# Input sums for the seven products read from an unsplit DRAM copy, two portions per step, in a macaron network on one Trainium2 core

## The chip, the cores and the metric

The kernel runs on one core of a Trainium2 chip. The metric is the device time of one execution in microseconds; lower is better. The engines appear under the names of the profile: PE (TensorE) multiplies, DVE (VectorE), ACT (ScalarE) and POOL (GpSimd) do elementwise work, SP (SyncE) issues most of the transfers, each engine in the order of its own instruction list.

## What is computed

Two layers over 512 tokens with a context of 256 tokens in front, 1024 features, all in fp32. Each layer is a gated FFN, a mixer, and a second gated FFN; each of the three is wrapped in a residual, a layer norm and a modulation by shift, scale and gate vectors. The mixer of layer 0 is a bidirectional gated linear attention plus a windowed pooling, that of layer 1 a differential attention.

```python
def ffn_substep(x, mods, w_in, w_out, g, b):
    shift, scale, gate = mods
    y = swiglu(modulate(x, shift, scale), w_in, w_out)
    return layer_norm(ALPHA * x + MACARON * gate * y, g, b)
def swiglu(h, w_in, w_out):
    a, b = jnp.split(h @ w_in, 2, axis=-1)
    return (jax.nn.silu(a) * b) @ w_out
```

w_in is 1024 x 5632 and w_out 2816 x 1024. The first three FFNs see 768 tokens, the last one only the 512 of the sequence.

## The kernel before, in words

The program is, in this order: FFN 1, the even mixer, FFN 2, FFN 3, the odd mixer, FFN 4. Features lie on the 128 partitions in 8 blocks, tokens along the free axis.

**Three matmuls for one product.** Every fp32 operand is split into a high part and a remainder, both in the fast fp32r form (`split`, L117 on ACT for the high part, L119 mostly on DVE, at some places on POOL, for the remainder), and `mm3` (L157 to L159) multiplies high by high, high by low, low by high. The tiles `xh`, `xl` hold the split input of the running stage.

**The FFN's input projection.** The 2816 hidden features make 11 double blocks. The first `plain` ones (4 with 768 tokens, 5 with 512) go through `project`, two units each, where PE multiplies all 8 feature blocks in the ordinary way: a first group of units together with the last steps of the layer norm before, then the rest one by one, and beside each of these the generator `after` is moved on by one step. The remaining blocks go through `seven`, a Strassen-like scheme: 7 products of half-size operands in place of 8, 84 matmuls per block with 384 or 256 columns. Its operands are sums of weight quarters (POOL, L669 to L680, then split on ACT and DVE) and sums of input quarters. The latter are what `after` makes, in 4 portions (`sums_of_inputs`, L634): three POOL adds put xh and xl together again (tiles `b`, L646), five DVE subtractions form the sums (L644, the first of them twice because xh and xl are subtracted one after the other), and three of the sums are split into the tiles `six` (ACT and DVE). No block can go through `seven` beyond its first product before all four portions are there.

**The output projection and the layer norm** (`out_phase`, `layer_norm`) treat the tokens in two halves. While PE runs half 1, the norm of half 0 is moved on between its steps: two `mean` calls (each sums two accumulators by two matmuls with a matrix of 1/1024, L476), a reciprocal root, and then for each of the 8 blocks j a multiplication on DVE (L329), the modulated `h` (ACT L336 and POOL L338), its split into xh and xl, and the residual kept for the next stage (POOL L344) and stored (SP). At the same time ACT and DVE split the output weights of half 1 (`spare<-raw`). The norm of half 1 is moved on in the next stage's `project`.

**Order.** A scheduler puts each engine's instructions in order when the kernel is built; buffers come from pools, and a transfer or an operation waits until its buffer is free.

Of the kernel before, what the change touches and what calls it, by code (L numbers as in the profile page):

```python
# [12 lines left out]
F32 = mybir.dt.float32  # L13
# [6 lines left out]
P = 128  # L20
D = 1024
KB = D // P
NCTX = 256
NLAT = 512
NT = NCTX + NLAT
# [17 lines left out]
class Net:  # L43
    def __init__(self, tc, ctx, ins, out):
        self.tc, self.nc, self.ins, self.out = tc, tc.nc, ins, out
        self.ctx = ctx
        nc = self.nc
        pool = lambda name, bufs, **k: ctx.enter_context(tc.tile_pool(name=name, bufs=bufs, **k))
        self.const = pool("const", 1)
        self.stream = pool("stream", 1)  # L50
        self.lnp = pool("lnp", 1)
        self.n = 0
        self.psum_cm = None
        self.open_psum(h=7, st=1)
# [12 lines left out]
        self.ones_d = c.tile([P, P], F32, name="ones_d")  # L67
        nc.vector.memset(self.ones_d, 1.0 / D)
        self.eps_ln = c.tile([P, 1], F32, name="eps_ln")
        nc.vector.memset(self.eps_ln, LN_EPS)  # L70
        self.eps_rms = c.tile([P, 1], F32, name="eps_rms")
        nc.vector.memset(self.eps_rms, RMS_EPS)
        self.ident = c.tile([P, P], F32, name="ident")
        make_identity(nc, self.ident)
        self.ln = c.tile([P, DEPTH, 3, 2, KB], F32, name="ln")
        self.bada = c.tile([P, DEPTH, N_MOD * KB], F32, name="bada")
        nc.scalar.dma_start(out=self.bada, in_=ins["b_ada"])
        nc.scalar.dma_start(out=self.ln, in_=ins["ln"])
        self.lb = self._lower_bound(c, self._load(c, "hg_lb", [P, 8]))
        self.RB = None  # L80
        self.ax = None
        self.mod = [
            [c.tile([P, N_MOD * KB], F32, name=f"mod_{l}_{v}") for v in range(2)] for l in range(DEPTH)
        ]
        self.c_bc = self.c_act = self.settled = None
# [138 lines left out]
    def start(self, pool):  # L224
# [33 lines left out]

        w = lambda q: [load(self.ins["w_ada0"][q, i]) for i in range(KB // 2)]
# [6 lines left out]
        for j in range(KB):  # L266
# [8 lines left out]
            self.split(self.xh[:, j, :], self.xl[:, j, :], x_)  # L275
            if j % 2 and q < 4:
                columns(q, quarter)
# [21 lines left out]
    def layer_norm(self, half, halves, aff, nxt, ax_new, r_of, s1, done, table):  # L299
        nc = self.nc  # L300
# [6 lines left out]
        pm = self.mean(s1, n)  # L307
# [12 lines left out]
        pv = self.mean(s2, n)  # L320
# [6 lines left out]
        for j in range(KB):  # L327
            r = r_of(half, j)
            nc.vector.tensor_mul(out=r, in0=r, in1=rs[:, :n])  # L329
            if nxt is not None:  # L330
# [8 lines left out]
                self.split(self.xh[:, j, c0:c1], self.xl[:, j, c0:c1], h[:, :n])  # L339
            g, b = aff[:, 0, j:j + 1], aff[:, 1, j:j + 1]  # L340
# [27 lines left out]
    def out_phase(self, pool, nk, wsrc, gload, halves, gate, l, i, nxt, r_of, table=None, keep=False, ada=iter(())):  # L368
# [5 lines left out]
        if nxt is not None:  # L374
            self.n += 1
            ax_new = self.dram.tile([P, KB, NT], F32, name=f"ax{self.n}")
        nh = nk // 2
# [95 lines left out]
    def mean(self, s, n):  # L473
        ps = self.ps("st")[:, :n]
        for i in range(2):
            self.nc.tensor.matmul(out=ps, lhsT=self.ones_d, rhs=s[i], start=i == 0, stop=i == 1)  # L476
        return ps

    def residual(self, r, j, c0, c1):
# [5 lines left out]
        nc.scalar.mul(out=r, in_=r, mul=ALPHA)  # L485

# [6 lines left out]
    def project(self, ws, halves, ps_of, done, group, early=None, spare=None, after=None):  # L493
# [40 lines left out]
        for x in range(group, len(ws)):  # L534
            w = ahead.pop(0)
            if after:
                next(after, None)
# [15 lines left out]
    def ffn(self, l, p, halves, nxt, ada=((), ()), table=None, first_of_all=False):  # L553
# [5 lines left out]
        plain = 4 if n > 512 else 5  # L559
        in_ada, out_ada = (list(a) for a in ada)  # L560
        with ExitStack() as st:
# [72 lines left out]
            def sums_of_inputs():  # L634

                t1 = [self.spare(pool)[:, :2 * m].rearrange("p (k c) -> p k c", k=2) for _ in range(2)]
# [3 lines left out]
                for k in range(4):  # L640
                    hi = lambda K, N: B(K, N)[0][:, k, :].bitcast(F32)
                    lo = lambda K, N: B(K, N)[1][:, k, :].bitcast(F32)
                    b12, b22, b21 = (self.tmp("b")[:, :m] for _ in range(3))
                    sub = lambda o, a, b: nc.vector.tensor_sub(out=o, in0=a, in1=b)  # L644
                    for t, q in ((b12, (0, 1)), (b22, (1, 1)), (b21, (1, 0))):
                        nc.gpsimd.tensor_add(out=t, in0=hi(*q), in1=lo(*q))  # L646
                    if k == 1:
                        made["next"] = ahead(plain, room(plain))
                    a = t1[k // 2][:, k % 2, :]
                    sub(a, b12, hi(0, 0))  # L650
                    sub(a, a, lo(0, 0))
# [125 lines left out]
    def even_mixer(self, nxt):  # L777
# [5 lines left out]
        with ExitStack() as st:  # L783
# [14 lines left out]
            def proj_head(h, group):  # L798
                tiles = {}
                kinds = ("ff", "fb", "q", "g")  # L800
                cols = (12 + h, 16 + h, h, 8 + h)
# [39 lines left out]
            def gla(h):  # L841
# [4 lines left out]
                q, sg, F = d["q"], d["g"], d["f"]  # L846
# [129 lines left out]
                nc.vector.tensor_mul(out=rec, in0=rec, in1=sg)  # L976
# [51 lines left out]
            for h in range(H):  # L1028
                gla(h)
                if h + 1 < H:  # L1030
                    proj_head(h + 1, 0)
            proj_u()
        self.open_psum(h=7, st=1)
        self.mixer_out(8, ins["w_out_even"], mixd, halves, (0, 5), 0, 1, nxt, (0, 1, 2, 3, 6, 7, 4, 5))
# [336 lines left out]
```

## Time and profile before

| | us |
|---|---|
| median of 3 runs | 2773.55 (2772.56 to 2774.47) |
| the profiled execution | 2768.34 |
| its span | 2766.6 |
| granted TensorE clock, mean | 0.991 |

The times of all rows below are of the profiled execution, counted from the start of its span; it lies 5.2 us below the median, and 1.7 us of its time are outside the span. The profile gives for every engine when it was busy, and in square brackets the idle time in front of an instruction with what ended it.

### The profile page before, as it was taken

The page shows a single profiled execution, that of the slowest core. Times are in us where ns is not written, and L with a number is a line of the kernel's source. Part 1 is how long each engine was busy: PE and PEld are TensorE (multiplying, and loading weights), DVE is VectorE, ACT ScalarE, POOL GpSimd, SP SyncE. Part 2 cuts the span into 40 slices and gives each one's busy share as a digit, 9 for nine tenths or more (in the row PEclk, how much of TensorE's full clock was granted, in tenths as well). Part 3 has the DMA queues.
Part 4 walks back from the last instruction along what each step waited for, and adds up shares of the span by engine and source line. Part 5 has one row for each costly group of instructions (what it writes and reads, how often), then busy time and mean ns, then how long its engine had stood idle before and what let it go on. Part 6 is the DMA issues. An engine that isn't in the chain of part 4 may idle for free.

```text
span 2766.6 us, 43965 instructions
## 1 busy us (share of the span) xinstructions
PE 2669.8 (97%) x17396; PEld 2430.9 (88%) x17396; DVE 1957.9 (71%) x2905; ACT 1215.3 (44%) x1918; POOL 897.0 (32%) x686
## 2 busy tenths in 40 slices
PE   8999999999999899999999999999999998999997
PEld 6999988987787789998898999988887777989997
DVE  4899677757774679977786775556727786677665
ACT  3433433544552533443354444423534555545553
POOL 1555300522110554440054544201422211465302
PEclk9999999999999999999999999999999999999998
DMA  6344266521114334426653432265521113323563
GB/s 257 130 144 134 92 234 232 192 99 64 45 38 167 108 115 146 140 92 225 217 202 131 155 124 77 103 220 199 187 77 46 39 35 100 126 93 119 176 213 117
DMA packets 138770, 374.20 MB, mean 135 GB/s; under 512 B 16066, under 2 KB 47170, under 8 KB 138564
## 3 DMA queue, kind: packets, MB, share of 16 engines
q1 hardware_dynamic: 136832, 370.21, 38.2%
q8 instruction: 136, 2.23, 0.3%
q10 hardware_dynamic: 1732, 1.20, 0.1%
q14 instruction: 70, 0.57, 0.1%
HBM read 337.78 MB, written 33.56 MB: 134 GB/s over the span
## 4 chain that ended last, share of the span: by engine, by line
PE 75%; DVE 11%; ACT 5%; POOL 4%; issue 3%; DMA 1%; SPq 0%; POOLq 0%; ACTq 0%; DVEq 0%
PE ps L157 22%; PE ps L158 22%; PE ps L159 22%; DVE r4l L119 1%; PE ps L1237 1%; PE ps L1238 1%; PE ps L1239 1%; DVE spare L644 1%; DVE b L644 1%; ACT r4h L117 1%; PE ps L1208 1%; PE ps L476 1%; PE pss L1136 1%; DVE spare L119 1%; POOL b L646 1%
## 5 line engine op out<-in xcount | busy, mean ns | idle before, releaser
L117 ACT CAST r4h<-raw 128x1024 fp32r<-128x1024 f32 (+1 forms) x322 | 332.6, 1035 | 626.0 <-PE ps L158 318.7
L157 PE MATMUL ps<-xh,r4h 128*128 128x512 f32 (+2 forms) x1732 | 583.2, 338 | 12.1 <-ACT xh L117 8.3
L159 PE MATMUL ps<-xh,r4l 128*128 128x512 f32 (+2 forms) x1732 | 579.4, 335 | 0.0
L158 PE MATMUL ps<-xl,r4h 128*128 128x512 f32 (+2 forms) x1732 | 578.6, 334 | 0.7 <-DVE xl L119 0.7
L119 DVE TENSOR_TENSOR r4l<-raw,r4h 128x1024 fp32r<-128x1024 f32 (+1 forms) x306 | 371.0, 1213 | 229.2 <-ACT r4h L117 168.3
L157 PEld LDWEIGHTS ps<-xh,r4h 128*128 128x128 f32 x1732 | 326.3, 189 | 42.5 <-ACT xh L117 11.5
L158 PEld LDWEIGHTS ps<-xl,r4h 128*128 128x128 f32 x1732 | 326.7, 189 | 22.8 <-DVE xl L119 2.8
L159 PEld LDWEIGHTS ps<-xh,r4l 128*128 128x128 f32 x1732 | 326.9, 189 | 20.7 <-issue 0.5
L157 PE MATMUL ps<-six,r4h 128*128 128x384 f32 (+1 forms) x852 | 279.8, 328 | 13.9 <-ACT c L708 13.8
L158 PE MATMUL ps<-six,r4h 128*128 128x384 f32 (+1 forms) x852 | 277.2, 325 | 0.0
L159 PE MATMUL ps<-six,r4l 128*128 128x384 f32 (+1 forms) x852 | 276.5, 325 | 0.0
L157 PE MATMUL ps<-r4h 128*128 128x512 f32 (+1 forms) x768 | 276.5, 360 | 0.0
L159 PE MATMUL ps<-r4h,r4l 128*128 128x512 f32 (+1 forms) x768 | 275.6, 359 | 0.2
L158 PE MATMUL ps<-r4l,r4h 128*128 128x512 f32 (+1 forms) x768 | 275.5, 359 | 0.0
L157 PE MATMUL ps<-r4h,spare 128*128 128x256 f32 (+1 forms) x896 | 263.6, 294 | 2.7 <-ACT spare L117 2.7
L159 PE MATMUL ps<-r4h,spare 128*128 128x256 f32 (+1 forms) x896 | 260.5, 291 | 4.2 <-DVE spare L119 4.1
L158 PE MATMUL ps<-r4l,spare 128*128 128x256 f32 (+1 forms) x896 | 260.6, 291 | 0.0
L680 POOL TENSOR_TENSOR raw<-raw,late 128x512 f32<-128x512 f32 x71 | 96.6, 1361 | 427.7 <-DVE r4l L119 427.7
L119 DVE TENSOR_TENSOR r4l<-late,r4h 128x1024 fp32r<-128x1024 f32 x71 | 105.7, 1489 | 121.4 <-PE ps L158 107.8
L159 PEld LDWEIGHTS ps<-r4h,spare 128*128 128x128 f32 x896 | 172.9, 193 | 7.7 <-DVE spare L119 5.4
L185 DVE SCALAR_TENSOR_TENSOR trash<-spare 128x1024 bf16<-128x1024 f32 x112 | 178.9, 1599 | 0.4 <-DMA spare<-in_w_ada 0.4
L157 PEld LDWEIGHTS ps<-r4h,spare 128*128 128x128 f32 x896 | 173.0, 193 | 7.0 <-ACT spare L117 3.3
(288 smaller groups left out, 5648.3 us busy)
## 6 DMA issues: line engine op xcount, KB each, us to landing
raw<-in_w_ffn_in SPq DMA_DIRECT2D x176, 512.0 KB, 3.5
raw<-in_w_ffn_out SPq DMA_DIRECT2D x176, 512.0 KB, 4.2
spare<-in_w_ada SPq DMA_DIRECT2D x80, 512.0 KB, 5.2
six<-in_w_ada SPq DMA_DIRECT2D x64, 512.0 KB, 5.6
g<-late_g SPq DMA_DIRECT2D x88, 128.0 KB, 2.1
six<-g SPq DMA_DIRECT2D x44, 256.0 KB, 4.5
raw<-in_w_in_even SPq DMA_DIRECT2D x20, 512.0 KB, 3.5
raw<-in_w_in_odd SPq DMA_DIRECT2D x16, 512.0 KB, 3.5
```

The costliest lines, as they stand in the source:

```text
L117: self.copied = self.nc.scalar.copy(out=h, in_=src)
L119: eng.tensor_sub(out=l, in0=src, in1=h.bitcast(F32))
L157: mm(out=ps, lhsT=h, rhs=xh, start=first, stop=False)
L158: mm(out=ps, lhsT=h, rhs=xl, start=False, stop=False)
L159: mm(out=ps, lhsT=l, rhs=xh, start=False, stop=last)
L185: nc.vector.scalar_tensor_tensor(out=self.tmp("trash").bitcast(BF16), in0=r, scalar=1.0, in1=self.c_bc[v], op0=ALU.mult, op1=ALU.mult, acc ...
L476: self.nc.tensor.matmul(out=ps, lhsT=self.ones_d, rhs=s[i], start=i == 0, stop=i == 1)
L644: sub = lambda o, a, b: nc.vector.tensor_sub(out=o, in0=a, in1=b)
L646: nc.gpsimd.tensor_add(out=t, in0=hi(*q), in1=lo(*q))
L680: nc.gpsimd.tensor_sub(out=a12, in0=a12, in1=sums[:, 512:])
L1136: mm(out=ps[:, half, :384], lhsT=Q[halfs[m], i, qs], rhs=K[halfs[m], j, ks], start=x == 0, stop=x == 2)
L1208: mm(out=po[:, qs], lhsT=v[:, c, h * P:(h + 1) * P], rhs=t[:, c, :], start=c == 0, stop=c == NC - 1)
```

## The change

FFN inputs get an unsplit copy in DRAM (`whole`), written by SP where the input is split: at the start, and in `layer_norm` behind each split of `h` (ahead of the store of the residual). `sums_of_inputs` reads its quarters back from it, 16 transfers per FFN, so that the 48 POOL adds and one DVE subtraction of each portion fall away. `project` moves `after` on by two steps per unit. `plain` falls by one, so one more block of each FFN goes through `seven`. `mean` adds the two accumulators on DVE first in the norm of half 0, and uses one matmul there. In the even mixer the gate projection of the last head comes after the pooling's projections, its gating is a function of its own, and the order in which the output projection takes its inputs is changed.

```diff
-        for i in range(2):
-            self.nc.tensor.matmul(out=ps, lhsT=self.ones_d, rhs=s[i], start=i == 0, stop=i == 1)
+        if not last:
+            self.nc.vector.tensor_add(out=s[0], in0=s[0], in1=s[1])
+            s = s[:1]
+        for i, part in enumerate(s):
+            self.nc.tensor.matmul(out=ps, lhsT=self.ones_d, rhs=part, start=i == 0, stop=i == len(s) - 1)
...
                 self.split(self.xh[:, j, c0:c1], self.xl[:, j, c0:c1], h[:, :n])
+                if whole is not None:
+                    nc.sync.dma_start(out=whole[:, j, c0:c1], in_=h[:, :n])
...
-            if after:
-                next(after, None)
+            for _ in range(2):
+                next(after or iter(()), None)
...
-        plain = 4 if n > 512 else 5
+        plain = 3 if n > 512 else 4
...
-                    for t, q in ((b12, (0, 1)), (b22, (1, 1)), (b21, (1, 0))):
-                        nc.gpsimd.tensor_add(out=t, in0=hi(*q), in1=lo(*q))
+                    for t, (K, N) in ((a, (0, 0)), (b12, (0, 1)), (b22, (1, 1)), (b21, (1, 0))):
+                        nc.sync.dma_start(out=t, in_=self.whole[:, K * 4 + k, cols[N]])
...
-                    sub(a, b12, hi(0, 0))
-                    sub(a, a, lo(0, 0))
+                    sub(a, b12, a)
...
                 if h + 1 < H:
-                    proj_head(h + 1, 0)
+                    gate(h)
+                if h + 2 < H:
+                    proj_head(h + 1, 0)
+                elif h + 1 < H:
+                    proj_head(h + 1, 0, ("ff", "fb", "q"))
             proj_u()
+            proj_head(H - 1, 0, ("g",))
+            gate(H - 1)
```

What the scheduler makes of it is seen in the engines' lists. First DVE in FFN 2, where the first group of units has ended; `raw`, `late`, `r4l`, `r4s` belong to the weights of the next seven-product blocks. Before:

```order
L119 TENSOR_TENSOR r4l<-raw,r4h 128x1024
L583 TENSOR_TENSOR late_g<-sil,ps 128x256 x2
L644 TENSOR_TENSOR spare<-b,xh 128x384 x2
L644 TENSOR_TENSOR spare<-spare,xl 128x384
L644 TENSOR_TENSOR b<-b 128x384
L644 TENSOR_TENSOR spare<-spare,xl 128x384
L644 TENSOR_TENSOR b<-b,spare 128x384
L119 TENSOR_TENSOR six<-b,six 128x384
L644 TENSOR_TENSOR b<-b 128x384
L119 TENSOR_TENSOR six<-b,six 128x384
L644 TENSOR_TENSOR b<-b 128x384
L119 TENSOR_TENSOR six<-b,six 128x384
```

The same place of the changed kernel, where L658 is the line of the subtractions and L593 and L597 are the gating:

```order
L119 TENSOR_TENSOR r4l<-raw,r4h 128x1024
L597 TENSOR_TENSOR late_g<-sil,ps 128x256 x2
L119 TENSOR_TENSOR r4l<-late,r4h 128x1024
L119 TENSOR_TENSOR r4s<-raw,r4s 128x512
L658 TENSOR_TENSOR spare<-b,spare 128x384
L119 TENSOR_TENSOR r4l<-raw,r4h 128x1024
L658 TENSOR_TENSOR b<-b 128x384
L658 TENSOR_TENSOR b<-b,spare 128x384
L658 TENSOR_TENSOR spare<-b,spare 128x384
L119 TENSOR_TENSOR six<-b,six 128x384
L658 TENSOR_TENSOR b<-b 128x384
L119 TENSOR_TENSOR six<-b,six 128x384
```

One block's weight splits are now in front of the input sums instead of in the middle, the sums are one subtraction shorter, and the `spare` of the sums holds a loaded quarter.

Next POOL at the same place of FFN 2, with `late`, `raw` for the weight sums. Before:

```order
L669 TENSOR_TENSOR late<-raw 128x512
L670 TENSOR_TENSOR late<-late,raw 128x512
L671 TENSOR_TENSOR raw<-raw 128x512
L646 TENSOR_TENSOR b<-xh,xl 128x384 x6
L680 TENSOR_TENSOR raw<-raw,late 128x512
L669 TENSOR_TENSOR late<-raw 128x512
L670 TENSOR_TENSOR late<-late,raw 128x512
L671 TENSOR_TENSOR raw<-raw 128x512
L646 TENSOR_TENSOR b<-xh,xl 128x384 x6
L119 TENSOR_TENSOR xl<-spare,xh 128x384 x4
```

And in the changed kernel (L681 to L692 are the weight sums, L119 the remainder of the fourth sum):

```order
L681 TENSOR_TENSOR late<-raw 128x512
L682 TENSOR_TENSOR late<-late,raw 128x512
L683 TENSOR_TENSOR raw<-raw 128x512
L692 TENSOR_TENSOR raw<-raw,late 128x512
L681 TENSOR_TENSOR late<-raw 128x512
L682 TENSOR_TENSOR late<-late,raw 128x512
L683 TENSOR_TENSOR raw<-raw 128x512
L119 TENSOR_TENSOR xl<-spare,xh 128x384 x2
L681 TENSOR_TENSOR late<-raw 128x512
L682 TENSOR_TENSOR late<-late,raw 128x512
L119 TENSOR_TENSOR xl<-spare,xh 128x384
L683 TENSOR_TENSOR raw<-raw 128x512
```

The runs of six adds of xh and xl are gone, and the weight sums of two blocks and the splits into `xl` have moved up into their place.

Last ACT in the output projection of FFN 3, half 1, where the norm's blocks (`xh<-h`) and the split of the output weights (`spare<-raw`) alternate. Before, from the first `xh` on:

```order
L117 CAST xh<-h 128x512
L336 ACTIVATE h<-six,aff 128x256 x2
L117 CAST xh<-h 128x512 x2
L336 ACTIVATE h<-six,aff 128x256
L117 CAST spare<-raw 128x1024
L117 CAST xh<-h 128x512
L336 ACTIVATE h<-spare,aff 128x256 x2
L117 CAST xh<-h 128x512 x2
L336 ACTIVATE h<-spare,aff 128x256
L117 CAST spare<-raw 128x1024
L117 CAST xh<-h 128x512
L117 CAST spare<-raw 128x1024
```

And in the changed kernel, from its first `xh` on:

```order
L117 CAST xh<-h 128x512 x2
L338 ACTIVATE h<-six,aff 128x256 x2
L117 CAST xh<-h 128x512 x2
L117 CAST spare<-raw 128x1024
L338 ACTIVATE h<-spare,aff 128x256
L117 CAST xh<-h 128x512
L338 ACTIVATE h<-spare,aff 128x256 x2
L117 CAST xh<-h 128x512 x2
L117 CAST spare<-raw 128x1024 x2
L338 ACTIVATE h<-spare,aff 128x256
L117 CAST r4h<-six 128x512
L117 CAST xh<-h 128x512
```

The second of the weight splits in this stretch stood behind the sixth `xh` and now stands behind the seventh; the first has moved from behind the third to behind the fourth.

## Rows read from the trace of the kernel before

**Rows 1.** the page, busy time, share and instructions by engine

```profile
PE 2669.8 (97%) x17396; PEld 2430.9 (88%) x17396; DVE 1957.9 (71%) x2905; ACT 1215.3 (44%) x1918; POOL 897.0 (32%) x686
```

**Rows 2.** PE timeline, end of the plain units in FFN 1: start, duration, instruction

```profile
94.39 0.40 PE L157 MATMUL ps<-xh,r4h 128*128 128x512 f32 x1
...
95.45 0.34 PE L157 MATMUL ps<-xh,r4h 128*128 128x384 f32 x1
95.62 0.34 PE L158 MATMUL ps<-xl,r4h 128*128 128x384 f32 x1
```

**Rows 3.** windows, PE: length, busy time (matmuls), clock, DMA share, GB/s

```profile
2460.00:2480.00 20.00, 20.00 (x169) 1.00 0.34 119
```

**Rows 4.** waits of PE: total us, times, longest

```profile
PE ps L476 <- DVE acc L471: 9.2, 5, 4.3
...
PE ps L1008 <- DVE KK L1003: 4.2, 1, 4.2
```

**Rows 5.** PE timeline, the first wait behind the plain units, FFN 1 to 4

```profile
102.28 0.44 PE L157 MATMUL ps<-six,r4h 128*128 128x384 f32 x1 [2.44 <-ACT c L708]
...
1007.65 0.69 PE L157 MATMUL ps<-six,r4h 128*128 128x384 f32 x1 [6.01 <-ACT c L708]
...
1539.55 0.44 PE L157 MATMUL ps<-six,r4h 128*128 128x384 f32 x1 [0.67 <-ACT c L708]
...
2446.78 0.58 PE L157 MATMUL ps<-six,r4h 128*128 128x256 f32 x1 [4.33 <-ACT c L708]
```

**Rows 6.** POOL timeline in FFN 2, the second run of adds

```profile
989.88 7.15 POOL L646 TENSOR_TENSOR b<-xh,xl 128x384 f32<-128x384 f32 x6
```

**Rows 7.** DVE timeline in FFN 2

```profile
975.67 0.54 DVE L644 TENSOR_TENSOR spare<-spare,xl 128x384 f32<-128x384 f32 x1
976.14 0.55 DVE L644 TENSOR_TENSOR b<-b,spare 128x384 f32<-128x384 f32 x1
...
994.78 1.37 DVE L644 TENSOR_TENSOR spare<-b,xh 128x384 f32<-128x384 f32 x1
```

**Rows 8.** DVE timeline, the weight split in front of the sums, FFN 1 to 4

```profile
58.66 1.22 DVE L119 TENSOR_TENSOR r4l<-raw,r4h 128x1024 fp32r<-128x1024 f32 x1
...
963.40 1.23 DVE L119 TENSOR_TENSOR r4l<-raw,r4h 128x1024 fp32r<-128x1024 f32 x1 [2.15 <-ACT r4h L117]
...
1500.64 1.81 DVE L119 TENSOR_TENSOR r4l<-raw,r4h 128x1024 fp32r<-128x1024 f32 x1 [7.77 <-ACT r4h L117]
...
2416.38 1.23 DVE L119 TENSOR_TENSOR r4l<-raw,r4h 128x1024 fp32r<-128x1024 f32 x1 [9.53 <-ACT r4h L117]
```

**Rows 9.** DVE timeline in FFN 4, a subtraction of 256 columns and the next

```profile
2420.17 0.41 DVE L644 TENSOR_TENSOR b<-b 128x256 f32<-128x256 f32 x1
2420.50 0.41 DVE L644 TENSOR_TENSOR spare<-spare,xl 128x256 f32<-128x256 f32 x1
```

**Rows 10.** PE timeline, the means of half 0, two matmuls (four records) each

```profile
497.27 1.88 PE L476 MATMUL ps<-acc,ones_d 128*128 128x512 f32 x4
...
909.09 1.98 PE L476 MATMUL ps<-acc,ones_d 128*128 128x512 f32 x4 [1.70 <-DVE acc L471]
...
2692.75 1.03 PE L476 MATMUL ps<-acc,ones_d 128*128 128x256 f32 x4
```

**Rows 11.** tile acc: min/median/max ns, first and last start, forms

```profile
L471 DVE TENSOR_TENSOR acc<-acc,spare x8: 411/678/681, 489.7 to 2689.3; 128x512 f32<-128x512 f32 x6, 128x256 f32<-128x256 f32 x2
```

**Rows 12.** PE timeline, output projection of FFN 3, half 1

```profile
1446.90 0.39 PE L157 MATMUL ps<-r4h,spare 128*128 128x256 f32 x1 [0.91 <-ACT spare L117]
...
1448.34 0.39 PE L159 MATMUL ps<-r4h,spare 128*128 128x256 f32 x1 [0.93 <-DVE spare L119]
```

**Rows 13.** ACT timeline, the same stretch

```profile
1445.82 1.03 ACT L117 CAST spare<-raw 128x1024 fp32r<-128x1024 f32 x1
1448.74 0.62 ACT L117 CAST xh<-h 128x512 fp32r<-128x512 f32 x1 [1.89 <-POOL h L338]
```

**Rows 14.** windows, the same stretch, columns as in the third group

```profile
1440.00:1460.00 20.00, 18.16 (x136) 0.91 0.63 218
```

More of the change, by code (lines that the diff above doesn't have):

```diff
@@ L79, in __init__ @@
         self.lb = self._lower_bound(c, self._load(c, "hg_lb", [P, 8]))
-        self.RB = None
+        self.RB = self.whole = None
         self.ax = None
@@ L257, in load @@
             return t
+        self.whole = self.whole_input()
         w = lambda q: [load(self.ins["w_ada0"][q, i]) for i in range(KB // 2)]
@@ L275, in start @@
             self.split(self.xh[:, j, :], self.xl[:, j, :], x_)
+            nc.sync.dma_start(out=self.whole[:, j, :], in_=x_)
             if j % 2 and q < 4:
@@ L299, in layer_norm @@
     def layer_norm(self, half, halves, aff, nxt, ax_new, r_of, s1, done, table):
-        nc = self.nc
+        nc, whole = self.nc, self.whole
         c0, c1 = halves[half]
@@ L306, in layer_norm @@
                 yield
-        pm = self.mean(s1, n)
+        pm = self.mean(s1, n, half)
         s2 = self.sums(n)
@@ L319, in layer_norm @@
             yield
-        pv = self.mean(s2, n)
+        pv = self.mean(s2, n, half)
         rs, rt = self.tmp("rs"), self.tmp("rt")
@@ L376, in out_phase @@
             ax_new = self.dram.tile([P, KB, NT], F32, name=f"ax{self.n}")
+        self.whole = self.whole_input() if nxt is not None and nxt[1] in (0, 6) else None
         nh = nk // 2
@@ L471, in add_up, with mean @@
             (self.nc.vector, self.nc.gpsimd)[j % 2].tensor_add(out=s[j % 2], in0=s[j % 2], in1=r)
-    def mean(self, s, n):
+    def mean(self, s, n, last):
         ps = self.ps("st")[:, :n]
-        for i in range(2):
-            self.nc.tensor.matmul(out=ps, lhsT=self.ones_d, rhs=s[i], start=i == 0, stop=i == 1)
+        if not last:
[3 more added lines that the diff above has]
+            self.nc.tensor.matmul(out=ps, lhsT=self.ones_d, rhs=part, start=i == 0, stop=i == len(s) - 1)
         return ps
@@ L485, in residual, with whole_input @@
         nc.scalar.mul(out=r, in_=r, mul=ALPHA)
+    def whole_input(self):
+        self.n += 1
+        return self.dram.tile([P, KB, NT], F32, name=f"whole{self.n}")
     def settle(self, steps=None):
@@ L640, in sums_of_inputs @@
                 for k in range(4):
-                    hi = lambda K, N: B(K, N)[0][:, k, :].bitcast(F32)
-                    lo = lambda K, N: B(K, N)[1][:, k, :].bitcast(F32)
+                    a = t1[k // 2][:, k % 2, :]
                     b12, b22, b21 = (self.tmp("b")[:, :m] for _ in range(3))
                     sub = lambda o, a, b: nc.vector.tensor_sub(out=o, in0=a, in1=b)
-                    for t, q in ((b12, (0, 1)), (b22, (1, 1)), (b21, (1, 0))):
-                        nc.gpsimd.tensor_add(out=t, in0=hi(*q), in1=lo(*q))
+                    for t, (K, N) in ((a, (0, 0)), (b12, (0, 1)), (b22, (1, 1)), (b21, (1, 0))):
+                        nc.sync.dma_start(out=t, in_=self.whole[:, K * 4 + k, cols[N]])
                     if k == 1:
                         made["next"] = ahead(plain, room(plain))
-                    a = t1[k // 2][:, k % 2, :]
-                    sub(a, b12, hi(0, 0))
-                    sub(a, a, lo(0, 0))
+                    sub(a, b12, a)
                     sub(b12, b22, b12)
@@ L796, in even_mixer, with proj_head @@
             half_of = lambda ap, i: ap[:, i * 384:(i + 1) * 384]
-            def proj_head(h, group):
+            def proj_head(h, group, kinds=("ff", "fb", "q", "g")):
                 tiles = {}
-                kinds = ("ff", "fb", "q", "g")
-                cols = (12 + h, 16 + h, h, 8 + h)
+                cols = [{"ff": 12, "fb": 16, "q": 0, "g": 8}[kind] + h for kind in kinds]
                 d = heads[h]
@@ L845, in gla @@
                 d = heads[h]
-                q, sg, F = d["q"], d["g"], d["f"]
+                q, F = d["q"], d["f"]
                 ev = lambda ap, m: ap.rearrange("p (n two m) -> p n two m", two=2, m=m)[:, :, 0, :]
@@ L975, in gla, with gate @@
                     nc.vector.scalar_tensor_tensor(out=r2, in0=po[b], scalar=nw, in1=r2, op0=ALU.mult, op1=ALU.mult)
-                nc.vector.tensor_mul(out=rec, in0=rec, in1=sg)
+                d["rec"] = rec
+            def gate(h):
+                rec = heads[h]["rec"]
+                nc.vector.tensor_mul(out=rec, in0=rec, in1=heads[h]["g"])
                 nc.sync.dma_start(out=mixd[:, h, :], in_=rec)
@@ L1030, in even_mixer @@
                 if h + 1 < H:
+                    gate(h)
+                if h + 2 < H:
                     proj_head(h + 1, 0)
+                elif h + 1 < H:
+                    proj_head(h + 1, 0, ("ff", "fb", "q"))
             proj_u()
+            proj_head(H - 1, 0, ("g",))
+            gate(H - 1)
         self.open_psum(h=7, st=1)
-        self.mixer_out(8, ins["w_out_even"], mixd, halves, (0, 5), 0, 1, nxt, (0, 1, 2, 3, 6, 7, 4, 5))
+        self.mixer_out(8, ins["w_out_even"], mixd, halves, (0, 5), 0, 1, nxt, (0, 1, 6, 7, 4, 5, 2, 3))
     def odd_mixer(self, nxt):
```

## The prediction

> **What bounds the kernel now.** I read the page first: PE is busy for 97% of the span and DVE for 71% [rows 1], so a change pays where it takes matmuls away or closes a gap on PE. Next I read the waits of PE and the PE timeline around them. Three kinds of gap touch this change. At the seam between the plain units and the seven products PE waits 2.44, 6.01, 0.67 and 4.33 us in the four FFNs, 13.45 us together; the row names the copy of the first product on ACT, but that copy stands behind the last input sums in ACT's list, so it is they that are late [rows 5]. In half 1 of an output projection it waits for a split of the output weights, 0.91 and 0.93 us in FFN 3, and the clock of that stretch falls to 0.91 [rows 12, 14]. It waits for the accumulators of the means, 9.2 us in all, and once 4.2 us for the pooling at the end of the even mixer [rows 4].
>
> **One block fewer in the plain way.** In a plain unit pair of 768 tokens, six matmuls of one feature block of a unit take from 94.39 to 95.45, that is 1.06 us; a double block has 16 such sixes, 17.0 us. A 384-column matmul follows the one before after 0.17 to 0.18 us (95.45 to 95.62), and I take 0.175: 84 of them are 14.7 us [rows 2]. Each of the first three FFNs saves 2.3 us of PE. In FFN 4 a window of seven products holds 169 matmuls in 20 us, 0.118 us each, so a block is 9.9 us; the plain block has 48 matmuls of 512 columns, which by the plain stretch less its 256-column part (1.06 / 3 - 0.118 = 0.235) are 11.3 us at most [rows 2, 3]. I take 1.0 saved, a little less, because a stretch of one width needs no change of width. Together 7.9 us, if the seams stay as they are.
>
> **They do not stay.** With two portions per unit, and one double block fewer, the sums have two plain units of cover (17.0 us) where they had four (34). So I work out when the fourth portion can be ready. In the changed order DVE has, from the first weight split behind the group of units: four weight splits of that kind (1.2 us each, one of them half as long, 4.2 us) and two small gating steps, together 4.8 us, then 16 subtractions and 12 remainders of 384 columns. Undisturbed these follow each other after 0.47 us (975.67 to 976.14) [rows 7], 13.2 us for 28. But the row at 994.78 took 1.37 us, as its neighbours did, while POOL ran its six adds from 989.88 on [rows 6, 7]: an operation of DVE that meets a POOL one loses some 0.8 us. The adds are gone, but POOL's list brings the weight sums of two blocks and two `xl` splits forward into the same time, about 11 operations, so I charge 11 x 0.8 = 8.5 us. Sum 26.5 us. The weight splits start at 58.66, 963.40, 1500.64 and 2416.38 [rows 8]. For FFN 1 to 3 this gives readiness at about 86 (there two output splits come between), 990 and 1527. In FFN 4 a subtraction takes 0.33 us (2420.17 to 2420.50) [rows 9], 28 of them 9.2, and with 4.8 and a smaller overlap of some 6 us it is 2436.
>
> From there PE has to run the block that was plain before as seven products, and only then is it where it restarted before: 86 + 14.7 = 100.7 against 102.28; 990 + 14.7 = 1004.7 against 1007.65; 1527 + 14.7 = 1541.7 against 1539.55; 2436 + 9.9 = 2445.9 against 2446.78 [rows 5]. Gains of 1.6, 2.9 and 0.9, a loss of 2.2: **3 us gained**. The lower bound: twice the overlap, 4 x 8 us later, less what PE waits already, is a loss of some 20, but the list does not hold that many POOL operations in 26 us; 3 us more at each seam is the worst I hold likely, -9. The upper bound: the sums come before PE needs them, then the 13.45 us of waiting and the 7.9 us of the blocks are both won, and 2 to 4 us of halved clock behind the two long waits: 24.
>
> **The reads and writes of the copy.** 56 writes and 64 reads on SP's queue. No row shows this traffic. The writes stand ahead of the residual's stores, nobody on the engines waits for those within the stage, and the reads are issued when the norm has ended, while the weight splits still stand in front of the first sum. I take nothing, and up to 2 us per FFN if the reads hold the weight loads back that are queued behind them; that is in the -9.
>
> **The means.** In half 0 of each norm one matmul with the 1/1024 matrix falls away, twice. A pair of 512 columns takes 1.88 us and one of 256 columns 1.03, the drain of the last included [rows 10], so one is at most 0.94 and 0.51; less the drain I take 0.86 and 0.43. Four norms have 512 columns (FFN 1 to 3 and the even mixer), two have 256: 8 x 0.86 + 4 x 0.43 = 8.6 us that PE spent and no longer spends. The added DVE addition takes 0.68 us (0.41 with 256 columns) [rows 11]. At 497.27 PE found the accumulators ready, with no bracket in the row; at 909.09 it waited 1.70 us for them [rows 10], and there the addition lengthens the wait. The same holds once in the odd mixer. I subtract 1.1: **7.5 us gained**. The bounds: all 12 additions on the path cost 8 x 0.68 + 4 x 0.41 = 7.1, leaving 1.5; none gives 8.6.
>
> **End of the even mixer.** The gate projection of the last head (48 matmuls, 8 sixes of 1.06, 8.5 us) now lies where PE waited 4.2 us for the pooling [rows 4], but it is missing as filler beside the last head's small matmuls, where DVE is late already. I put the two against each other and keep **1 us gained**, between -3 (the whole filler turned into a wait, less the 4.2) and +6 (the wait and its halved clock both gone).
>
> **Output weights in half 1.** Here the scheduler moved the splits. In FFN 3 the second weight split stood behind the sixth `xh`, at 1445.82; it now stands behind the seventh, which in this trace starts at 1448.74 because POOL's `h` comes late [rows 13]. If the seventh `xh` stays where it is, the split ends 3.5 us later, and PE, which waited 0.91 for it [rows 12], waits that much longer; the wait of 0.93 for the next split goes into it. Net 2.5 us, in FFN 1 and FFN 3 alike, and in FFN 2, where the new writes to DRAM are in the same stretch, perhaps 4.5: 9.5 us at most likely. If POOL gives `h` earlier, since its list there is reordered too, nothing. I take half: **5 us lost**, between 0 and 14.
>
> **Sum.** 3 + 7.5 + 1 - 5 = 6.5 us faster. The profiled 2768.34 would become 2761.8, and the median, which lies 5.2 above it, 2767.0. A measurement of this kernel can tell about 0.2%, 5.5 us, from no change; the forecast lies just beyond it.
>
> **The rivals.**
> *The sums are hidden.* For it: half of DVE's contention came from the adds that go; against it: POOL has other work queued and ready, and the rows of the adds show that DVE pays for any of it. The chain would be 13.2 + 4.8 = 18 us against 17.0 of cover, the seams would bring up to 24 instead of 3, and the time would be 2746. The page "GPSIMD Engine Reference" of the Trainium skill (Key points) says that GpSimd shares its SBUF interfaces with VectorE and contends with DVE instructions that have two SBUF inputs. Read by itself it speaks for this rival, since 12 POOL operations per FFN are gone: 12 x 0.8 = 10 us off each chain, as the time above has it; the trace agrees with the page on who collides, and the lists show that others take the place.
>
> *No change.* The sums come 2 to 3 us later than I have it at each seam, behind reads that are late or more POOL work, or the means' additions fall on the path: the 6.5 is used up, 2773 give or take 5. For it: DVE ends every seam's chain, and its cover is halved.
>
> *Slower by the weight splits.* Each output projection with a delayed split waits 6 us or more instead of 2, and the clock falls as it fell at 1440 to 1460, to 0.91 for the window, which is 20 x 0.09 = 1.8 us [rows 14]. It decides when the three together cost over 17 us, that is 5.7 each, since 11.5 are gained elsewhere; at 7 each it is 21, and the time 2783. For it: PE there has no other work, half 1 being the end of the stage; against it: the norm's blocks need only to come 3 us sooner for the wait to vanish. The Trainium skill's "TensorE: Matmul & The Clock Gate" (HAM oscillation) has the clock fall to its lower level, 1.2 GHz, behind long waits for transfers, and says nothing of waits as short as these; by it alone the 1.8 us would be left out, and the 7 would be 5.2, not enough to be slower. The window shows the fall behind two waits under 1 us, so I keep it.
>
> **How the numbers follow.** Forecast 0.45, of which 0.35 lie beyond 0.2% and 0.10 within; sums hidden, wholly or in good part, 0.19, all faster; no change 0.17, nearly all within; weight splits 0.19, slower. Faster 0.54, same 0.26, slower 0.20. The forecast's own range is 2760 to 2773, from the half-widths of the seams and the splits. For 8 in 10 I leave out the upper end of the hidden case and the worse half of the slower one: 2752 to 2779.
>
> **What the profile would show.** Right: 7 products begin at about 86, 990, 1527 and 2436 with waits of 4 to 6 us in front, named for ACT `c` or `six`; L476 has 36 matmuls for 48, and PE's busy time falls by some 16 us; no wait of 4 us is left at the end of the even mixer; the weight-split waits in the output projections are 2 to 4 us longer. Wrong, if the seams show no wait, if a load of weights behind the copy's reads is what PE waits for, or if the output projections take 6 us longer each.

## The result and the profile after

The changed kernel is slower: 2786.14 us (2782.32 to 2791.18) against 2772.56, five executions of each, a ratio of 1.0059 with a 95% interval of 1.0048 to 1.0071. I had forecast 2767, so size and sign are wrong, and the time lies outside 2760 to 2773 and outside 2752 to 2779. One execution of those below, the profiled one of e1, took 5229 us and is left out of every comparison. The changed kernel's profiled execution took 2782.32, its span is 2780.5, 13.9 us longer than before.

The page of the changed kernel, busy time by engine, answers [rows 1]:

```profile
PE 2659.5 (96%) x17372; PEld 2434.3 (88%) x17372; DVE 1976.0 (71%) x2924; ACT 1232.0 (44%) x1940; POOL 861.2 (31%) x654
```

PE is busy for 10.3 us less (I had forecast some 16), and the kernel is still longer: PE waits more. Where it waits can be read off the PE timeline: I took the start of the first or last matmul of each stage in both traces, and the difference of the differences is what each stage lost.

| stage | later (+) or earlier (-), us |
|---|---|
| FFN 1, up to the last seven-product matmul | +7.5 |
| FFN 1, output projection | -0.9 |
| even mixer up to its output projection | +4.1 |
| even mixer, output projection | -3.4 |
| FFN 2, input projection | +3.3 |
| FFN 2, output projection | +0.7 |
| FFN 3, input projection | +1.9 |
| FFN 3, output projection | +1.2 |
| odd mixer with its output projection | -1.8 |
| FFN 4, input projection | +2.1 |
| FFN 4, output projection | -0.8 |

The four input projections lose 14.8 us, more than the whole difference. The seams, in the PE timeline of the changed kernel, answer [rows 5]:

```profile
82.68 0.34 PE L159 MATMUL ps<-xh,r4l 128*128 128x384 f32 x1
89.44 0.69 PE L157 MATMUL ps<-six,r4h 128*128 128x384 f32 x1 [6.42 <-ACT c L720]
...
93.22 0.44 PE L157 MATMUL ps<-six,r4h 128*128 128x384 f32 x1 [0.53 <-ACT six L117]
...
94.69 0.44 PE L158 MATMUL ps<-six,r4h 128*128 128x384 f32 x1 [1.03 <-DVE six L119]
...
1001.90 0.69 PE L157 MATMUL ps<-six,r4h 128*128 128x384 f32 x1 [9.88 <-ACT c L720]
...
1536.38 0.44 PE L157 MATMUL ps<-six,r4h 128*128 128x384 f32 x1 [4.04 <-ACT c L720]
...
2447.73 0.38 PE L157 MATMUL ps<-six,r4h 128*128 128x256 f32 x1 [4.32 <-ACT c L720]
...
2450.41 0.58 PE L157 MATMUL ps<-six,r4h 128*128 128x256 f32 x1 [0.70 <-ACT six L117]
...
2453.93 0.58 PE L158 MATMUL ps<-six,r4h 128*128 128x256 f32 x1 [1.66 <-DVE six L119]
```

The matmul at 89.44 is the first of the third product. The first two products read `xh` and `xl` alone and need no sums, so PE had run both of them (24 matmuls, the last at 82.68) before it stopped; the description of the kernel before, which lets only one product go ahead of the sums, is one short. The third product reads the sums (`six`) and adds to the result of the first, so it also needs ACT's copy of that result (`c`), for which the row is named.

The first waits of the four seams are 24.7 us together, where [rows 5] had 13.45, and in FFN 1 and FFN 4 PE runs into the unfinished sums again: 3.9 us more in four waits named for `six`. The DVE timeline of FFN 2 shows what it waited for; it answers [rows 7, 8]:

```profile
970.74 1.98 DVE L119 TENSOR_TENSOR r4l<-raw,r4h 128x1024 fp32r<-128x1024 f32 x1 [2.59 <-ACT r4h L117]
...
976.79 1.56 DVE L119 TENSOR_TENSOR r4s<-raw,r4s 128x512 fp32r<-128x512 f32 x1 [1.83 <-ACT r4s L117]
978.28 1.64 DVE L658 TENSOR_TENSOR spare<-b,spare 128x384 f32<-128x384 f32 x1
979.84 2.31 DVE L119 TENSOR_TENSOR r4l<-raw,r4h 128x1024 fp32r<-128x1024 f32 x1
...
984.07 0.55 DVE L658 TENSOR_TENSOR b<-b 128x384 f32<-128x384 f32 x1
984.53 0.55 DVE L119 TENSOR_TENSOR six<-b,six 128x384 fp32r<-128x384 f32 x1
...
991.82 3.15 DVE L119 TENSOR_TENSOR six<-b,six 128x384 fp32r<-128x384 f32 x2
994.89 2.88 DVE L658 TENSOR_TENSOR b<-b 128x384 f32<-128x384 f32 x2
...
1001.50 0.56 DVE L119 TENSOR_TENSOR six<-b,six 128x384 fp32r<-128x384 f32 x1
```

POOL in the same stretch:

```profile
968.98 1.29 POOL L681 TENSOR_TENSOR late<-raw 128x512 f32<-128x512 f32 x1 [4.63 <-DMA ax<-late]
...
971.60 2.28 POOL L683 TENSOR_TENSOR raw<-raw 128x512 f32<-128x512 f32 x1
973.84 2.27 POOL L692 TENSOR_TENSOR raw<-raw,late 128x512 f32<-128x512 f32 x1
...
977.89 1.61 POOL L682 TENSOR_TENSOR late<-late,raw 128x512 f32<-128x512 f32 x1
...
986.60 4.88 POOL L119 TENSOR_TENSOR xl<-spare,xh 128x384 fp32r<-128x384 f32 x2 [5.53 <-ACT xh L117]
991.43 1.59 POOL L681 TENSOR_TENSOR late<-raw 128x512 f32<-128x512 f32 x1
```

From 970.74 to the end of the last remainder at 1001.97 are 31.2 us; I had 26.5. Where POOL is idle (984.07, 984.53) the operations follow each other after 0.47 us, as in [rows 7]; beside POOL's `xl` splits and weight sums two of them take 2.9 to 3.2 us. The window from the first sum to the last remainder says the same, with busy times of PE, PEld, DVE, ACT and POOL (instructions), clock, DMA share and GB/s:

```profile
978.28:1001.97 23.69, 13.81 (x79) 12.25 (x77) 23.59 (x31) 9.57 (x21) 14.74 (x9) 0.83 0.43 146
```

DVE is busy in 23.59 of 23.69 us. Its 28 sums and remainders, one weight split and one gating step would take 13.2 + 1.2 + 0.6 = 15 us undisturbed; the other 8.6 us go with nine POOL operations, almost 1 us each.

### The profile page after: what moved, and what is told of

The parts are those of the page before. It is cut to its first block, busy times and chain, and to the rows that moved or that the text cites. A ratio compares the mean times of both kernels' runs of the same rounds, so it can differ in the third digit from the quotient of the medians.

```text
span 2780.5 us, 44176 instructions
## 1 busy us (share of the span) xinstructions
PE 2659.5 (96%) x17372; PEld 2434.3 (88%) x17372; DVE 1976.0 (71%) x2924; ACT 1232.0 (44%) x1940; POOL 861.2 (31%) x654
## 4 chain that ended last, share of the span: by engine, by line
PE 75%; DVE 10%; issue 7%; ACT 4%; POOL 3%; DMA 1%; SPq 0%; POOLq 0%; DVEq 0%; ACTq 0%
PE ps L157 22%; PE ps L158 22%; PE ps L159 22%; PE ps L1258 1%; PE ps L1259 1%; PE ps L1260 1%; DVE r4l L119 1%; DVE b L658 1%; DVE six L119 1%; PE ps L1229 1%; PE pss L1157 1%; ACT e L1161 1%; DVE late L935 1%; POOL h L340 1%; PE ps L485 1%
## 5 line engine op out<-in xcount | busy, mean ns | idle before, releaser
L157 PE MATMUL ps<-xh,r4h 128*128 128x384 f32 (+2 forms) x1668 | 560.8, 338 | 12.5 <-ACT xh L117 8.7
L158 PE MATMUL ps<-xl,r4h 128*128 128x384 f32 (+2 forms) x1668 | 558.1, 335 | 0.4 <-DVE xl L119 0.4
L159 PE MATMUL ps<-xh,r4l 128*128 128x384 f32 (+2 forms) x1668 | 558.0, 335 | 0.0
L119 DVE TENSOR_TENSOR r4l<-raw,r4h 128x1024 fp32r<-128x1024 f32 (+1 forms) x306 | 374.0, 1224 | 236.7 <-ACT r4h L117 165.8
L157 PEld LDWEIGHTS ps<-xh,r4h 128*128 128x128 f32 x1668 | 315.9, 190 | 39.3 <-ACT xh L117 11.1
L158 PEld LDWEIGHTS ps<-xl,r4h 128*128 128x128 f32 x1668 | 316.6, 190 | 19.3 <-DVE xl L119 1.6
L159 PEld LDWEIGHTS ps<-xh,r4l 128*128 128x128 f32 x1668 | 316.4, 190 | 18.5 <-issue 0.9
L157 PE MATMUL ps<-six,r4h 128*128 128x384 f32 (+1 forms) x900 | 297.4, 330 | 28.7 <-ACT c L720 27.5
L158 PE MATMUL ps<-six,r4h 128*128 128x384 f32 (+1 forms) x900 | 294.7, 327 | 2.7 <-DVE six L119 2.7
L159 PE MATMUL ps<-six,r4l 128*128 128x384 f32 (+1 forms) x900 | 293.9, 327 | 0.0
L692 POOL TENSOR_TENSOR raw<-raw,late 128x512 f32<-128x512 f32 x75 | 98.9, 1319 | 465.5 <-DVE r4l L119 462.2
L119 DVE TENSOR_TENSOR r4l<-late,r4h 128x1024 fp32r<-128x1024 f32 x75 | 119.2, 1590 | 127.6 <-PE ps L158 123.8
L157 PEld LDWEIGHTS ps<-six,r4h 128*128 128x128 f32 x900 | 171.9, 191 | 34.4 <-ACT c L720 32.3
```

The source lines that it names most:

```text
L119: eng.tensor_sub(out=l, in0=src, in1=h.bitcast(F32))
L157: mm(out=ps, lhsT=h, rhs=xh, start=first, stop=False)
L158: mm(out=ps, lhsT=h, rhs=xl, start=False, stop=False)
L159: mm(out=ps, lhsT=l, rhs=xh, start=False, stop=last)
L692: nc.gpsimd.tensor_sub(out=a12, in0=a12, in1=sums[:, 512:])
```

## The experiments

All ratios are to the kernel before, with 95% intervals.

**e1, plain back.** The changed kernel with four and five plain blocks again:

```diff
-        plain = 3 if n > 512 else 4
+        plain = 4 if n > 512 else 5
```

> The changed kernel with plain put back to 4 and 5, all else as changed. Theory (the lost cover is the cause: DVE needs 31 us for the four portions and has two plain units, 17 us, to do it in): with four units of cover the waits at the four seams fall to under 2 us each, the 13 us of before are gone too, and the kernel is about 17 us faster than before (2755). Rival (the copy itself, its 120 transfers or the new order, makes the sums late whatever the cover): the waits stay at 4 to 10 us and the time stays at 2780 or more.

Measured: 2758.05 us, 0.9953 (0.9934 to 0.9971): 28 us faster than the changed kernel and faster than before. How the seams look with the longer cover is read from e5, e6 and e8. The rival is out: the copy does not make the sums late by itself.

**e2, the means alone**, on the kernel before:

```diff
+        if not last:
+            self.nc.vector.tensor_add(out=s[0], in0=s[0], in1=s[1])
+            s = s[:1]
...
```

> The kernel before with the change of the means alone. Its ACT list already has the output weight splits behind the 4th, 7th, 7th, 8th xh as in the changed kernel. Theory (the means save 1.7 us in each norm of 512 columns on PE, and the delayed weight splits give 1.3 to 3 us back in FFN 1 to 3): 1 to 3 us faster than before, with waits of 1.3, 1.5 and 2.1 us in each output projection. Rival (the splits are late because of the writes of the copy in the same stretch): 7 us faster, with the short waits of before.

Measured: 2768.25 us, 0.9991 (0.9981 to 1.0000). Between nothing and 5 us gained. Waits of PE from 1440 to 1480 us, which [rows 12] showed as 0.91 and 0.93:

```profile
PE ps L159 <- DVE spare L119: 3.1, 2, 1.9
PE ps L157 <- ACT spare L117: 1.3, 1, 1.3
```

The splits are late with the means alone and without the copy. In its trace the half 1 of FFN 1 to 3 is 0.9 to 1.2 us longer than before, although two matmuls of 0.86 us are gone.

**e3, the even mixer alone**, on the kernel before:

```diff
...
+                elif h + 1 < H:
+                    proj_head(h + 1, 0, ("ff", "fb", "q"))
             proj_u()
+            proj_head(H - 1, 0, ("g",))
+            gate(H - 1)
...
```

> The kernel before with the change of the even mixer alone. Theory (the gate projection is missing as filler beside the last head's small matmuls, and one more table load and a later mix write come with it): 2 to 3 us slower than before, with a wait of 2.7 us in the last head at about 800 us and none of 4 us at its end. Rival, my forecast: 1 us faster.

Measured: 2772.89 us, 1.0009 (0.9999 to 1.0018), so 2.5 us slower, at the edge of what can be told. Waits of PE from 780 to 860 us:

```profile
PE ps L932 <- DVE KK L923: 2.5, 1, 2.5
PE ps L874 <- DVE late L857: 1.5, 1, 1.5
PE ps L157 <- DVE g L823: 1.1, 1, 1.1
```

The wait of 4.2 us in [rows 4] is gone, and others have come in its place.

**e4, the block without the copy**, on the kernel before:

```diff
-        plain = 4 if n > 512 else 5
+        plain = 3 if n > 512 else 4
...
-            if after:
-                next(after, None)
+            for _ in range(2):
+                next(after or iter(()), None)
```

> The kernel before with plain lowered to 3 and 4 and two portions per step, without the copy: the POOL adds and the second subtraction stay. Theory (cover against length of the chain): the chain is longer by four subtractions and twelve collisions with POOL, some 10 us per FFN, so the waits at the seams are 12 to 20 us each and the kernel is 20 to 40 us slower than the changed one. Rival (the copy is what hurts, the block is won): 8 us faster than before.

Measured: 2807.15 us, 1.0127 (1.0109 to 1.0146), 21 us slower than the changed kernel by the medians and 19 by the ratios (the changed kernel has the means and the even mixer's part too, small by e2 and e3). Its waits of PE for the copy of the first product:

```profile
PE ps L157 <- ACT c L708: 52.3, 9, 16.3
```

The first waits at the four seams are 12.9, 16.3, 12.1 and 7.8 us; only that of FFN 4 is under the 12 that I expected. So the copy is worth some 20 us at this `plain`, and the step to 3 and 4 is what costs.

**e5, plain back and the even mixer as before.** The edit of e1, and `even_mixer` from the kernel before.

> The changed kernel with plain back at 4 and 5 and the even mixer as before; the copy, two portions per step and the means stay. Theory (cover; the even mixer's part costs 2 to 3 us): 2 to 3 us faster than with the changed even mixer, about 0.993 of the kernel before. Rival (the even mixer's part is worth nothing or gains when it stands in the changed kernel): the same 0.995 or more.

Measured: 2752.92 us, 0.9942 (0.9928 to 0.9957). That is 5 us under e1 by the medians and 3 by the ratios, and the two intervals overlap, so it shows little by itself; with e3 it speaks against the even mixer's part. Its trace has no wait at the four seams.

**e6, the copy and two portions per step alone**: e5 with the means as before too.

> Only the copy and two portions per step, on the kernel before: plain 4 and 5, means and even mixer as before. Theory (cover): the seam waits of 13 us fall to under 4 in all and with them the halved clock behind them, 0.994 of before; the output weight splits wait 2 us per FFN as before unless the copy's writes delay them too. Rival (the writes of the copy hurt the output projections or the reads hold the weights back): 0.997 or more, with waits for weights or splits longer than before.

Measured: 2754.90 us, 0.9946 (0.9934 to 0.9958). None of the waits at the four seams is left. All that PE waits for that copy in FFN 1 comes at 164 us, 64 us behind the seam (waits of PE from 60 to 180 us):

```profile
PE ps L157 <- ACT c L717: 0.2, 1, 0.2
```

In its trace the four input projections are 16 us shorter than before (1.8, 8.6, 1.8 and 3.8). The output projection of FFN 2, where the copy is written in half 1, is 2.9 us longer; those of FFN 1 and 3, without such writes, stay within 0.1 in half 1.

**e7, POOL's weight sums cut to 16 columns**, on the changed kernel. The products are of other weights: `sums` holds loaded weights, and the sums are formed in 16 columns only.

```diff
-                nc.gpsimd.tensor_add(out=s1, in0=a21, in1=a22)
+                nc.sync.dma_start(out=sums, in_=ws[2 * x])
+                e = slice(0, 16)
+                nc.gpsimd.tensor_add(out=s1[:, e], in0=a21[:, e], in1=a22[:, e])
...
-                nc.gpsimd.tensor_sub(out=a12, in0=a12, in1=sums[:, 512:])
+                nc.gpsimd.tensor_sub(out=a12[:, :16], in0=a12[:, :16], in1=sums[:, 512:528])
```

> The changed kernel, with the weight sums on POOL cut to 16 columns; the sums tile is loaded instead (so the products of the seven are of other weights). Theory (DVE's chain is 31 us rather than 18 because POOL's operations beside it stretch it): the chain falls to 20 to 24 us, the four seam waits of 25 us together fall by 15 or more, and the kernel comes out at about 2765. Rival (the chain is long because of ACT's splits or the reads from DRAM): the waits stay and so does the time, 2780 or more.

Measured: 2751.63 us, 0.9933 (0.9913 to 0.9953), by two executions, 34 us under the changed kernel. DVE in FFN 2:

```profile
960.45 1.23 DVE L119 TENSOR_TENSOR r4l<-raw,r4h 128x1024 fp32r<-128x1024 f32 x1 [2.60 <-ACT r4h L117]
...
966.74 0.56 DVE L658 TENSOR_TENSOR spare<-b,spare 128x384 f32<-128x384 f32 x1
967.22 1.22 DVE L119 TENSOR_TENSOR r4l<-raw,r4h 128x1024 fp32r<-128x1024 f32 x1
...
984.70 0.56 DVE L119 TENSOR_TENSOR six<-b,six 128x384 fp32r<-128x384 f32 x1
```

and the waits of PE for the copy of the first product:

```profile
PE ps L157 <- ACT c L722: 7.3, 4, 3.4
```

From the first sum to the last remainder 966.74 to 985.17 are 18.4 us where the changed kernel has 23.7; with the weight splits 24.7 for 31.2. The waits for that copy, 27.5 us in eight waits in the changed kernel, fall to 7.3 in four. What is left of the excess over 15 us lies mostly beside the `xl` splits, which still run on POOL. I had expected 2765. By the trace the four input projections are 30.7 us shorter than in the changed kernel; 20.6 of these are waits at the seams and some 5 are time at the lower clock behind them. The cut also brings the weight sums themselves earlier, which this run does not part from the lighter load on DVE; the durations in the rows above show the latter.

**e8, one portion per step**: e1 with the loop over two steps taken out.

> The changed kernel with plain back at 4 and 5 and one portion per step as before. Theory (it matters when the last portion may start): the fourth portion comes with the fourth unit, the waits at the seams are 3 to 8 us each as before, and the time is that of the kernel before within 0.2%. Rival (the copy alone takes the waits away, since the adds and subtractions are gone): as fast as with two portions, 0.995.

Measured: 2758.49 us, 0.9957 (0.9945 to 0.9970). My theory failed here: with the fourth portion beside the last unit the sums are in time too. In FFN 2 the last remainder is over at 995.3 where it was at 1003.0 in the kernel before, and PE does not wait at any of the four seams. What ended the waits of before is the copy, which takes work off POOL and DVE, and not the earlier start.

**e9, one matmul for the first mean only**: e6, and the addition in half 0 for the mean but not for the variance. ACT's list then keeps the splits where they were.

```diff
-        pv = self.mean(s2, n, half)
+        pv = self.mean(s2, n, 1)
```

> The copy and two portions per step, plain 4 and 5, the even mixer as before, and of the means only the first of the two in half 0 by one matmul (the second keeps two). ACT's list then has the output weight splits of half 1 where they were before (behind the 3rd, 6th, 7th xh) and not one xh later. Theory (the change of the means is worth its matmuls where the splits do not move): half 1 of each output projection is about 0.9 us shorter than with the old means, with split waits of 0.9 us as before and none of 1.9; some 3 us faster than the copy alone, 0.993 of the kernel before. Rival (the means give nothing since PE then waits for DVE in their place): half 1 as long as with the old means, 0.9945.

Measured: 2751.51 us, 0.9935 (0.9921 to 0.9948), the fastest, though not told apart from e5 and e6 by its time. By its trace half 1 of FFN 1 to 3 is 0.95, 1.45 and 0.95 us shorter than in e6, one matmul or a little more, and the waits from 525 to 560 us are those of before:

```profile
PE ps L159 <- DVE spare L119: 0.9, 1, 0.9
PE ps L157 <- ACT spare L117: 0.9, 1, 0.9
```

## Why the prediction was wrong

**The step that failed** is the readiness of the fourth portion under "They do not stay". DVE's chain does decide, and POOL's next weight sums do collide with it. But the term was mis-sized, and its consequences were left out.

- **The chain.** I had it at 26.5 us, 20 in FFN 4; it took 31.4, 31.2, 27.3 and 26.6 us. In FFN 2 it starts where I had it (970.74 is 963.40 plus the 7.2 us by which the stage began later), and my price held: 13 POOL operations lay beside it where I counted 11, and they cost 10.7 us, 0.8 each on average (8.6 by the nine beside the sums, 2.1 by the four beside the weight splits in front of them). Left out were the two more, the wait of 1.83 us for a weight part, and a gating step between the sums. In FFN 1 the chain also starts 5.4 us later than in the row that I took, at 64.08 for 58.66, behind two other weight splits for which I had counted less than 1 us. The first split of FFN 1 and the last remainders of FFN 1, 3 and 4:

```profile
64.08 1.65 DVE L119 TENSOR_TENSOR r4l<-raw,r4h 128x1024 fp32r<-128x1024 f32 x1
...
95.02 0.55 DVE L119 TENSOR_TENSOR six<-b,six 128x384 fp32r<-128x384 f32 x1
...
1537.47 1.03 DVE L119 TENSOR_TENSOR six<-b,six 128x384 fp32r<-128x384 f32 x1
...
2454.68 0.43 DVE L119 TENSOR_TENSOR six<-b,six 128x256 fp32r<-128x256 f32 x1
```

Allowing for the later start of each stage (0, 7.2, 11.3 and 12.7 us), the fourth portion was ready 9.5, 4.7, 0.2 and 6.4 us later than I had it. FFN 3 alone came out as forecast, with 1.9 us lost for 2.2.

- **The restart.** I took PE's restart for the readiness of all four portions. PE restarts when ACT has copied the first product, and in FFN 1 and 4 that copy stands ahead of the last casts of the sums, in FFN 1 so:

```profile
88.92 0.47 ACT L720 COPY c<-ps 128x384 f32<-128x384 f32 x1
...
94.20 0.51 ACT L117 CAST six<-b 128x384 fp32r<-128x384 f32 x1 [1.03 <-DVE b L658]
```

So PE restarted there without the fourth portion and stopped again, the 3.9 us in four waits.

- **The clock.** I took the clock behind the seam to cost what it had cost before. FFN 1 restarts in the changed kernel at 0.81 and 0.85 (windows, columns as in the window above); in FFN 2 PE runs 10 matmuls in 3 us at the lower level, 1.2 GHz:

```profile
80.00:90.00 10.00, 3.58 (x20) 3.26 (x19) 9.96 (x14) 4.65 (x10) 5.80 (x5) 0.81 0.69 225
90.00:100.00 10.00, 8.41 (x38) 7.33 (x37) 9.35 (x10) 5.66 (x9) 4.97 (x4) 0.85 0.61 215
```

```profile
1002.00:1005.00 3.00, 3.00 (x10) 0.50 0.46 152
```

By the clock in the traces PE multiplied at that level for some 20 us behind the four seams, and for 10 in the kernel before. A 384-column matmul follows the one before it after 0.32 us there (1002.38 to 1002.70) and after 0.175 at the full level, so I estimate that this costs some 4.5 us more than before.

The parts nearly add up: 15.1 us more of waiting at the seams (24.7 and 3.9 for 13.45), some 4.5 by the clock, 2.5 more in later waits for the same copy, less the 7.9 of the blocks, is 14 of the 14.8 us.

I had 3 us gained here, and -9 as the worst. None of the three signs by which I would have called the forecast wrong appeared, although it was wrong: a first wait well over the 4 to 6 us that I named, as the 9.9 of FFN 2, should have been one of them. That the sums can be hidden is shown by e5, e6 and e8, with the longer cover and not with the shorter one.

**A misreading of [rows 5].** I took the waits of the kernel before to be waits for late sums. In its FFN 1 ACT casts the last of them from 94.85 on, DVE's last remainder is over at 96.9, and PE stops at 99.84; between those casts and the copy ACT works through 5.7 us of weight splits, `xh` casts and other things:

```profile
94.85 1.18 ACT L117 CAST six<-b 128x384 fp32r<-128x384 f32 x2 [0.42 <-DVE b L644]
...
95.40 1.49 DVE L119 TENSOR_TENSOR six<-b,six 128x384 fp32r<-128x384 f32 x3
...
101.75 0.48 ACT L708 COPY c<-ps 128x384 f32<-128x384 f32 x1
```

In FFN 3 and 4, too, the sums are there before PE stops, and in FFN 2 they come 1.3 us behind it, of a wait of 6.01. The sums are one of several things that ACT has to get through ahead of the copy.

**What I did not weigh** is that the copy and the smaller `plain` are two changes with opposite signs. The block is worth 7.9 us by the count of its matmuls; its 17 us of cover are worth more, for giving up the one and taking back the other in e1 gains 28 us. And the copy with the old cover ends the 13 us of waits [rows 5], which I named only in an upper bound of the whole. By the ratios the copy gains 15 us at the old `plain` (e6), the smaller `plain` loses 35 without the copy (e4), and both together, with the rest of the change, lose 16. e1 and e8 agree.

**The means and the weight splits**: 7.5 gained and 5 lost, net 2.5, agrees with e2, which has 2.5 (0 to 5). The second part was too small, though: PE's waits that are named for splits into `spare` are 15.0 us in the whole of the changed kernel and 7.6 before, 7.4 more. That the splits move with the added addition and not with the copy I had left open; e2 shows it, and e9 that a mean is worth its matmul where they stay. One error of mine: [rows 12 to 14] are of the output projection of FFN 2, which I called FFN 3 (the ACT lists shown are those of FFN 3; the three lists place the splits alike). In the same stretch the changed kernel waits like this on PE:

```profile
1453.28 0.39 PE L159 MATMUL ps<-r4h,spare 128*128 128x256 f32 x1 [1.17 <-DVE spare L119]
...
1457.51 0.39 PE L157 MATMUL ps<-r4h,spare 128*128 128x256 f32 x1 [1.33 <-ACT spare L117]
...
1459.95 0.39 PE L159 MATMUL ps<-r4h,spare 128*128 128x256 f32 x1 [1.94 <-DVE spare L119]
```

4.4 us instead of 1.8, 2.6 more, which is what I had (2.5) before I halved the sum; the 4.5 that I had set for FFN 2 did not come.

**The end of the even mixer**: +1 was of the wrong sign, within its bounds. The wait of 4.2 us did go, and the first 6 us of the output projection, which had run at a clock of 0.72 (844 to 850), run at 1.00 (855 to 861). But the stage up to there is 4.1 us longer, with new waits beside the last head; e3, where only this was edited, shows the same ones. That the gate projection is missing there as filler fits them, and is not shown by itself.

**The copy's traffic**, taken as nothing: nearly so. e6 shows 2.9 us in FFN 2's half 1, whether from the writes or from an order that moved with them is open.

**The rivals.** It ended on the slower side, by the mechanism of "no change" (sums later than I had them) and not by the weight splits that I had priced for it. What stays open is the odd mixer, 1.8 us shorter in the changed kernel and between 4.6 shorter and 1.8 longer in the traces of e2 to e6, where at most its means and the writes of the copy were edited; that may be variation between executions.

## What to carry to other kernels

Work taken off one engine is not cover for another: before an edit shortens the stretch of matmuls that hides a chain, lay the chain out with everything that the second elementwise engine will run beside it, count a collision for every one of its operations, weight splits included, and check in the changed list where the chain starts. When a change bundles a relief (the copy) with a spending of the relief (one block less), price them one by one, and the arrangement that keeps the cover is a candidate of its own. A wait that a row names for one instruction may belong to what stands ahead of it in that engine's list; look at which of these ended last. An edit that looks local, such as one addition, can move the split of some weights in an engine's list; compare the lists ahead of the sum.

## What the runs showed of the hardware

A DVE operation beside POOL operations was slower by more than I had from [rows 7]: two remainders of 384 columns took 3.15 us for 1.0, a weight split of 1024 columns 2.31 for 1.23. POOL was slowed as well: a sum of 512 columns that took 1.29 us at 968.98, with DVE idle, took 2.28 at 971.60. In these rows the one that began later looks as if it waited for the end of the other and then took its usual time: that POOL sum ends at 973.88, 1.2 us behind the DVE split that began at 970.74, and DVE's subtraction at 978.28 ends 0.4 us behind the POOL sum that began at 977.89.

The granted clock did not follow the waits as I thought. The stretch with waits of 0.91 and 0.93 us in the kernel before shows 0.91 [rows 14]; the changed kernel, with 1.17, 1.33 and 1.94 us in the same place, shows 1.00, and e2, with the same three waits 5 us earlier, again 0.91 (windows of PE, the changed kernel and e2):

```profile
1450.00:1490.00 40.00, 34.88 (x224) 1.00 0.59 214
1440.00:1460.00 20.00, 15.56 (x114) 0.91 0.56 190
```
